# Compressed keys and values: the first layer's product in split fp32r, its weights through the shared stream

## The chip, the core and the metric

The program runs on one core of a Trainium2 chip. Its time is the device time of one execution in microseconds (us); several executions are timed and their median is given. Three runs of the kernel before gave a median of 3503.91 us (3499.05 to 3507.26).

A core has a matrix engine (TensorE; PE in the rows, with its weight loads as PEld), three engines for element-wise work (VectorE = DVE, ScalarE = ACT, GpSimd = POOL) and a queue engine (SyncE = SP) that here only issues DMAs. Each engine works through its own list of instructions in order, and an instruction that waits holds up all that stand behind it on that engine.

## The reference, cut to what matters

The program computes three layers in a row: two of a recurrent block with four kinds of mixing, and one attention layer. The change lies in the attention layer, at the place where keys and values are compressed into 15 blocks of 32 tokens:

```python
def compress(t, pe, w1, w2):
    blk = t[:, cidx] + pe[None, None, :, None, :]            # 15 blocks x 32 tokens, 4 groups
    blk = blk.transpose(0, 1, 3, 2, 4).reshape(B, n_c, G, CMP_BLOCK * dh)   # 32 x 64 = 2048 wide
    return jax.nn.gelu(blk @ w1) @ w2                        # w1: 2048 x 256, w2: 256 x 64
kc = partial_rope(compress(k_cmp, pe_ck, w_ck1, w_ck2), pos[:, cmp_end])
vc = compress(v_cmp, pe_cv, w_cv1, w_cv2)
```

`k_cmp` and `v_cmp` are two of fifteen slices of the projection `h @ w_in`. `kc` is used as extra key columns of a later attention, and `vc` as its values. The first product, `blk @ w1`, is 60 rows (4 groups x 15 blocks) by 2048 by 256, once for the keys and once for the values.

## The kernel before

**Weights.** Nearly all the products run in fp32r, a format with fewer bits than fp32. To keep the precision each operand is split into a rounded part hi and a remainder lo, and the products hi\*hi, hi\*lo and lo\*hi are summed. Activations are split once. Weights are split as they stream in, by `Core.prep` (line 82): SP loads half a megabyte into one of 3 buffers `raw` (line 102), ACT rounds it into one of 4 buffers `hi` (line 108), and DVE subtracts into one of 4 buffers `lo` (line 112). The buffers are handed out in the order in which the program calls `prep`, so the stream of weights has one order, and whoever uses a set of weights holds its buffers until then.

**Who uses the stream around the change.** Lines 174 to 176 (`stream_a`, weights as the stationary operand, 48 matmuls of 256 or 258 columns for one set of 128 outputs) and lines 225 to 227 (`stream_b`, activations stationary, 192 matmuls of 512 columns for 512 outputs over all 2048 inputs). In `block2` eight `stream_a` jobs come first and leave eight tiles `early0` to `early7`, the first four of which are `k_cmp` and `v_cmp`. Then the normalised input is split into `uq` (lines 1869 to 1871; POOL and DVE multiply into `tmp`, ACT rounds, DVE subtracts). Then come, in the order of the program: the tables for the rotary embedding (`tables`: `pos` is loaded into `pi`, DVE works out the angles at lines 1674 to 1706, ACT takes the sines at line 1705), the compression, two `stream_b` jobs for the values `vb` of the dilated attention, and the `stream_a` jobs for its queries and keys.

**Compression.** For keys and for values: ACT copies the four groups into a tile `cst` (lines 1787 and 1788, eight copies), the position term `pe` is loaded from ACT's queue (line 1790), and DVE adds it into the blocks `cbl` (line 1797, eight additions), a tile of 128 x 64 x 16, in which the 64 columns of one step j stand 16 elements apart. The weights `w1` come by ACT's queue as fp32 into buffers of their own, `cwk` and `cwv` (two each), 16 loads of 256 KB at line 1803. Line 1806 multiplies in plain fp32: for each of 16 steps j, 64 stationary columns of keys into the upper half of one PSUM bank and 64 of values into the lower half. The rest, lines 1809 to 1824, is gelu, a transposition and the second layer.

**The order of instructions.** The order on each engine isn't the order of the text. A scheduler inside the framework simulates the program and puts instructions of the engines in the order in which they become ready there, within what the data and the buffers allow. So in the program before line 1806 is spread over PE's list: 8 matmuls behind the two `vb` jobs, and 24 in small pieces between the matmuls of the next three `stream_a` jobs.

Of the kernel before, what the change touches and what calls it, by code (L numbers as in the profile page):

```python
# [9 lines left out]
F32 = mybir.dt.float32  # L10
F32R = mybir.dt.float32r
I32 = mybir.dt.int32
AF = mybir.ActivationFunctionType
OP = mybir.AluOpType
# [1696 lines left out]
class Attn:  # L1711
# [66 lines left out]
    def compress(self, xs):  # L1778

        nc, K = self.nc, self.K  # L1780
        bls = []
        for n, x in zip("kv", xs):
            st = self.t([128, 4, 256], "cst", 1)
            for g in range(4):
                src = x[g // 2]
                r = slice(64 * (g % 2), 64 * (g % 2) + 64)
                nc.scalar.copy(st[0:64, g], src[r, 0:256])
                nc.scalar.copy(st[64:128, g, 0:255], src[r, 1:256])
            pe = self.t([128, 16], "pe", 2)
            nc.scalar.dma_start(pe, self.A[f"pec{n}"])  # L1790
            bl = self.t([128, 64, 16], "cbl", 2)
            nc.gpsimd.memset(bl[:, 60:64], 0.0)
            for g in range(4):
                a = st[:, g, 0:240].rearrange("p (c j) -> p c j", j=16)[:, :, 0:16:2]
                b = st[:, g, 16:256].rearrange("p (c j) -> p c j", j=16)[:, :, 0:16:2]
                for h, v in enumerate((a, b)):
                    nc.vector.tensor_tensor(bl[:, 15 * g:15 * g + 15, 8 * h:8 * h + 8], v, pe[:, 8 * h:8 * h + 8].unsqueeze(1).to_broadcast([128, 15, 8]), op=OP.add)
            bls.append(bl)
        bank = K.g()
        for j0 in range(0, 16, 2):  # L1800
            w1 = [self.t([128, 2, 256], f"cw{n}", 2) for n in "kv"]
            for n, w in zip("kv", w1):
                nc.scalar.dma_start(w, self.A[f"wc{n}1"][:, j0:j0 + 2])
            for j in range(j0, j0 + 2):
                for i in range(2):
                    nc.tensor.matmul(bank[64 * i:64 * i + 64, 0:256], bls[i][:, :, j], w1[i][:, j - j0], start=(j == 0), stop=(j == 15))
        both = self.t([128, 4, 256], "cst", 1)
        x, u = both[:, 0], both[:, 1]
        nc.vector.tensor_copy(x, bank[:, 0:256])
        nc.vector.tensor_tensor(u, x, x, op=OP.mult)  # L1810
        nc.vector.tensor_tensor(u, u, x, op=OP.mult)
        nc.vector.scalar_tensor_tensor(u, u, 0.044715, x, op0=OP.mult, op1=OP.add)
        nc.scalar.activation(u, u, AF.Tanh, scale=math.sqrt(2.0 / math.pi))
        nc.vector.tensor_scalar(u, u, 0.5, 0.5, op0=OP.mult, op1=OP.add)
        nc.vector.tensor_tensor(x, x, u, op=OP.mult)
        for m in range(2):
            nc.tensor.transpose(bank[:, 256 + m * 128:384 + m * 128], x[:, m * 128:(m + 1) * 128], K.ident)
        hid = self.t([128, 2, 2, 64], "chid")
        nc.scalar.copy(hid, bank[:, 256:512].rearrange("p (m i c) -> p m i c", m=2, i=2))
        w2 = []  # L1820
        for n in "kv":
            w2.append(self.t([128, 2, 64], f"cw2{n}"))
            nc.scalar.dma_start(w2[-1], self.A[f"wc{n}2"])
        return hid, w2
# [330 lines left out]
```

## Time and profile before

| | before |
|---|---|
| time, median of 3 runs | 3503.91 us (3499.05 to 3507.26) |
| time of the profiled execution | 3503.24 us |
| its span, first to last instruction | 3501.4 us |
| PE busy | 3460.7 us (99%) |
| DVE busy | 2381.8 us (68%) |
| ACT busy | 1749.0 us (50%) |
| POOL busy | 492.8 us (14%) |
| DMA | 657.48 MB, mean 188 GB/s |
| granted clock of TensorE, mean | 0.994 |

Matmuls are pipelined: a row of the timeline gives a matmul's start and its own length, and the next one starts before it is over. What a matmul costs in a dense stretch is therefore the distance between two starts, not the length. The granted clock is given as a share of 2.4 GHz, so that 0.50 is 1.2 GHz. "Idle before" of a row is the time its engine did nothing ahead of it, and the arrow names what ended it. A line of the kernel before and the same line of the changed kernel differ by up to 7 in number, since the change adds 7 lines.

### The profile page before, as it was taken

The numbers are of one execution on the slowest core, as the hardware profiler recorded it, in microseconds if no ns is written. First come the engines' busy times: TensorE is split into PE (matmuls) and PEld (weight loads), VectorE is DVE, ScalarE is ACT, GpSimd is POOL, SyncE is SP. The second block draws the span as 40 slices with busy tenths as digits, with TensorE's granted clock in tenths as the row PEclk, the third lists the DMA queues.
The fourth block names the chain that finished last, engine by engine and source line by source line (L and its number), as shares of the span: only waits on it lengthen the run. The fifth ranks groups of instructions, "written<-read, shape, count | busy, mean of one in ns | idle before, by whom it ended". The sixth has DMA issues, their size and how long they took to land.

```text
span 3501.4 us, 58741 instructions
## 1 busy us (share of the span) xinstructions
PE 3460.7 (99%) x22403; PEld 2978.7 (85%) x22403; DVE 2381.8 (68%) x4330; ACT 1749.0 (50%) x2890; POOL 492.8 (14%) x686
## 2 busy tenths in 40 slices
PE   9999999999999999999999999999999999999998
PEld 8878888888888888888897888888888899988887
DVE  7776875777776546887785777776545766765554
ACT  5654544544444445655454544444345544554443
POOL 2122310211110001121320111111000112100000
PEclk9999999999999999999999999999999999999999
DMA  6334555666766665424456666666665545445555
GB/s 217 116 115 148 172 181 171 232 235 235 240 235 227 213 194 178 156 80 156 163 173 192 198 235 235 238 236 233 219 195 172 191 156 169 139 130 188 186 187 177
DMA packets 208554, 657.48 MB, mean 188 GB/s; under 512 B 24256, under 2 KB 27632, under 8 KB 208272
## 3 DMA queue, kind: packets, MB, share of 16 engines
q1 hardware_dynamic: 165952, 577.84, 50.6%
q10 hardware_dynamic: 42320, 75.89, 6.5%
q8 instruction: 176, 2.88, 0.3%
q14 instruction: 106, 0.87, 0.1%
HBM read 650.99 MB, written 2.65 MB: 187 GB/s over the span
## 4 chain that ended last, share of the span: by engine, by line
PE 95%; DVE 3%; ACT 1%; DMA 1%; issue 1%; POOL 0%; ACTq 0%; DVEq 0%; SPq 0%; POOLq 0%
PE s L178 23%; PE s L179 11%; PE s L225 8%; PE s L226 8%; PE s L227 8%; PE s L174 5%; PE s L175 5%; PE s L176 5%; PE g L225 4%; PE g L227 4%; PE g L226 4%; PE g L178 1%; PE g L175 1%; PE g L174 1%; PE g L176 1%
## 5 line engine op out<-in xcount | busy, mean ns | idle before, releaser
L112 DVE TENSOR_TENSOR lo<-raw,hi 128x1024 fp32r<-128x1024 f32 (+1 forms) x1089 | 1384.8, 1273 | 882.4 <-ACT hi L108 878.0
L108 ACT CAST hi<-raw 128x1024 fp32r<-128x1024 f32 (+1 forms) x1089 | 1139.5, 1049 | 1298.7 <-PE s L178 352.5
L178 PE MATMUL s<-uq,hi 128*128 128x512 f32 x3168 | 1111.4, 393 | 3.2 <-DVE e L276 3.2
L179 PE MATMUL s<-uq,lo 128*128 128x256 f32 x3168 | 884.2, 279 | 0.0
L178 PEld LDWEIGHTS s<-uq,hi 128*128 128x128 f32 x3168 | 593.6, 187 | 145.5 <-ACT hi L108 3.6
L179 PEld LDWEIGHTS s<-uq,lo 128*128 128x128 f32 x3168 | 593.7, 187 | 0.2
L174 PE MATMUL s<-uq,hi 128*128 128x256 f32 x1440 | 416.9, 290 | 5.2 <-ACT v L1512 2.5
L176 PE MATMUL s<-uq,lo 128*128 128x256 f32 x1440 | 416.0, 289 | 0.0
L175 PE MATMUL s<-uq,hi 128*128 128x256 f32 x1440 | 415.4, 288 | 0.0
L174 PEld LDWEIGHTS s<-uq,hi 128*128 128x128 f32 x1440 | 275.3, 191 | 14.3 <-issue 5.7
L175 PEld LDWEIGHTS s<-uq,hi 128*128 128x128 f32 x1440 | 275.1, 191 | 6.9 <-issue 6.1
L176 PEld LDWEIGHTS s<-uq,lo 128*128 128x128 f32 x1440 | 275.0, 191 | 6.8 <-issue 6.0
L226 PE MATMUL s<-lo,uq 128*128 128x512 f32 x672 | 269.4, 401 | 1.5 <-DVE lo L112 1.5
L227 PE MATMUL s<-hi,uq 128*128 128x512 f32 x672 | 267.8, 400 | 0.0
L225 PE MATMUL s<-hi,uq 128*128 128x512 f32 x672 | 266.5, 402 | 0.6 <-DVE k L1342 0.4
L444 POOL TENSOR_TENSOR gs<-e,R 128x256 f32<-128x256 f32 x88 | 77.8, 884 | 750.8 <-DVE e L276 412.9
L226 PEld LDWEIGHTS s<-lo,uq 128*128 128x128 f32 x672 | 127.4, 190 | 32.6 <-DVE lo L112 3.3
L225 PEld LDWEIGHTS s<-hi,uq 128*128 128x128 f32 x672 | 127.2, 189 | 32.0 <-issue 1.7
L227 PEld LDWEIGHTS s<-hi,uq 128*128 128x128 f32 x672 | 127.1, 189 | 30.0 <-issue 1.2
L225 PE MATMUL g<-hi,hid 128*128 128x512 f32 x352 | 139.2, 396 | 0.0
L226 PE MATMUL g<-lo,hid 128*128 128x512 f32 x352 | 139.2, 396 | 0.0
L227 PE MATMUL g<-hi,hid 128*128 128x512 f32 x352 | 139.2, 396 | 0.0
(639 smaller groups left out, 5311.2 us busy)
## 6 DMA issues: line engine op xcount, KB each, us to landing
raw<-in_wd_dram SPq DMA_DIRECT2D x176, 512.0 KB, 3.9
raw<-in_wg_dram SPq DMA_DIRECT2D x168, 512.0 KB, 4.1
raw<-in_wu_dram SPq DMA_DIRECT2D x168, 512.0 KB, 4.5
raw<-in_wina_dram SPq DMA_DIRECT2D x154, 512.0 KB, 3.8
raw<-in_win2a_dram SPq DMA_DIRECT2D x130, 512.0 KB, 3.6
raw<-in_winb_dram SPq DMA_DIRECT2D x96, 512.0 KB, 3.6
raw<-in_wout_dram SPq DMA_DIRECT2D x96, 512.0 KB, 3.9
aw<-in_wada_dram ACTq DMA_DIRECT2D x192, 256.0 KB, 4.4
```

The costliest lines, as they stand in the source:

```text
L108: self.last_hi = nc.scalar.copy(hi[:, :n], raw[:, :n])
L112: self.last = nc.vector.tensor_tensor(lo[:, :n], raw[:, :n], hi[:, :n].bitcast(F32), op=OP.subtract)
L174: nc.tensor.matmul(banks[i][:, 0:n], wh, x[:, 0:n], start=first, stop=False)
L175: nc.tensor.matmul(banks[i][:, 0:n], wh, x[:, n:2 * n], start=False, stop=False)
L176: nc.tensor.matmul(banks[i][:, 0:n], wl, x[:, 0:n], start=False, stop=last)
L178: nc.tensor.matmul(banks[i], wh, x, start=first, stop=False)
L179: nc.tensor.matmul(banks[i][:, 0:256], wl, x[:, 0:256], start=False, stop=last)
L225: nc.tensor.matmul(banks[tt], xh, wh, start=(i + j == 0), stop=False)
L226: nc.tensor.matmul(banks[tt], xh, wl, start=False, stop=False)
L227: self.last_mm = nc.tensor.matmul(banks[tt], xl, wh, start=False, stop=(end and j == 1))
L444: nc.gpsimd.tensor_tensor(g, e, rget(), op=OP.mult)
```

## The change

Four things change, all in `compress`:

- The weights `w1` no longer have buffers of their own. `K.prep` takes them, four steps j at a time: 4 sets for the keys and 4 for the values, of 512 KB each, through SP's queue and the buffers `raw`, `hi` and `lo`.
- The blocks are split as well: ACT copies `cbl`, rounded, into one half of a new tile `cb` (its name in the code is `hl`) and DVE subtracts into the other half. Both read `cbl` through the view `p c j -> p j c`, so with elements 16 apart, and write runs of 64. hi and lo of a step stand side by side as 128 stationary columns.
- For each step j there are two matmuls in fp32r, one with the hi of the weights and one with their lo, into a bank each for keys and for values: 2 x 32 in all. The upper half of the bank then holds what the blocks' hi gives and the lower half what their lo gives, and ACT and DVE add the halves together afterwards.
- Keys and values are done one after the other, where before all blocks were made first. `cbl` now has one buffer where it had two, and so has `cb`.

```diff
--- before.py
+++ after.py
@@ -1778,8 +1778,9 @@
     def compress(self, xs):
 
         nc, K = self.nc, self.K
-        bls = []
-        for n, x in zip("kv", xs):
+        banks = [K.g(), K.g()]
+        for i, n in enumerate("kv"):
+            x = xs[i]
             st = self.t([128, 4, 256], "cst", 1)
             for g in range(4):
                 src = x[g // 2]
@@ -1788,25 +1789,31 @@
                 nc.scalar.copy(st[64:128, g, 0:255], src[r, 1:256])
             pe = self.t([128, 16], "pe", 2)
             nc.scalar.dma_start(pe, self.A[f"pec{n}"])
-            bl = self.t([128, 64, 16], "cbl", 2)
+            bl = self.t([128, 64, 16], "cbl", 1)
             nc.gpsimd.memset(bl[:, 60:64], 0.0)
             for g in range(4):
                 a = st[:, g, 0:240].rearrange("p (c j) -> p c j", j=16)[:, :, 0:16:2]
                 b = st[:, g, 16:256].rearrange("p (c j) -> p c j", j=16)[:, :, 0:16:2]
                 for h, v in enumerate((a, b)):
                     nc.vector.tensor_tensor(bl[:, 15 * g:15 * g + 15, 8 * h:8 * h + 8], v, pe[:, 8 * h:8 * h + 8].unsqueeze(1).to_broadcast([128, 15, 8]), op=OP.add)
-            bls.append(bl)
-        bank = K.g()
-        for j0 in range(0, 16, 2):
-            w1 = [self.t([128, 2, 256], f"cw{n}", 2) for n in "kv"]
-            for n, w in zip("kv", w1):
-                nc.scalar.dma_start(w, self.A[f"wc{n}1"][:, j0:j0 + 2])
-            for j in range(j0, j0 + 2):
-                for i in range(2):
-                    nc.tensor.matmul(bank[64 * i:64 * i + 64, 0:256], bls[i][:, :, j], w1[i][:, j - j0], start=(j == 0), stop=(j == 15))
+
+            hl = self.t([128, 16, 2, 64], "cb", 1, F32R)
+            y = bl.rearrange("p c j -> p j c")
+            nc.scalar.copy(hl[:, :, 0], y)
+            nc.vector.tensor_tensor(hl[:, :, 1], y, hl[:, :, 0].bitcast(F32), op=OP.subtract)
+            for j0 in range(0, 16, 4):
+                hi, lo = K.prep([self.A[f"wc{n}1"][:, j0:j0 + 4].rearrange("p j c -> p (j c)")], 1024)
+                for j in range(4):
+                    for w in (hi, lo):
+                        nc.tensor.matmul(banks[i][:, 0:256], hl[:, j0 + j].rearrange("p a c -> p (a c)"), w[:, j * 256:(j + 1) * 256],
+                                         start=(j0 + j == 0 and w is hi), stop=(j0 + j == 15 and w is lo))
         both = self.t([128, 4, 256], "cst", 1)
         x, u = both[:, 0], both[:, 1]
-        nc.vector.tensor_copy(x, bank[:, 0:256])
+        for i in range(2):
+            R, Q = slice(64 * i, 64 * i + 64), slice(64 - 64 * i, 128 - 64 * i)
+            nc.scalar.copy(x[R], banks[i][Q, 0:256])
+            nc.vector.tensor_tensor(x[R], x[R], banks[i][R, 0:256], op=OP.add)
+        bank = banks[0]
         nc.vector.tensor_tensor(u, x, x, op=OP.mult)
         nc.vector.tensor_tensor(u, u, x, op=OP.mult)
         nc.vector.scalar_tensor_tensor(u, u, 0.044715, x, op0=OP.mult, op1=OP.add)
```

The scheduler then orders the instructions anew. On PE the list behind the last of the eight early `stream_a` jobs (lines 174 to 176 with 258 columns) went on with the first `vb` job (lines 225 to 227):

```order
L174 MATMUL s_27992<-u1_27386,hi_28024 128x258
L175 MATMUL s_27992<-u1_27386,hi_28024 128x258
L176 MATMUL s_27992<-u1_27386,lo_28025 128x258
L225 MATMUL s_28404<-hi_28407,uq_28057 128x512
L226 MATMUL s_28404<-lo_28408,uq_28057 128x512
L227 MATMUL s_28404<-hi_28407,uq_28057 128x512
```

At the same place all 64 new matmuls now stand (line 1808), first the 32 of the keys into bank `g_28211`, then the 32 of the values into `g_28212`, and the first `vb` job behind them; of each run of 32 the first two are shown:

```order
L176 MATMUL s_27992<-u1_27386,lo_28025 128x258
L1808 MATMUL g_28211<-hi_28238,cb_28234 128x256
L1808 MATMUL g_28211<-lo_28239,cb_28234 128x256
...
L1808 MATMUL g_28212<-hi_28318,cb_28314 128x256
L1808 MATMUL g_28212<-lo_28319,cb_28314 128x256
...
L225 MATMUL s_28462<-hi_28465,uq_28057 128x512
```

The compression's matmuls moved ahead of the 192 matmuls of `vb` (two banks of 96) that they stood behind, and no longer come in pieces. SP's list agrees: the eight loads of `w1` stand directly behind those of the early jobs and ahead of the 16 loads of `win2b`, which are the weights of `vb`.

On ACT, the stretch from the last instruction of the split of `uq` (line 1870) to the first copy of the blocks (line 1787) read as follows before; `hi<-raw` are the weights of `vb`, `vo` its result:

```order
L1870 ACTIVATE uq<-tmp,ada_94 128x256
L1670 DMA pi<-in_pos_dram 128x256
L1672 DMA ri<-in_c_rope_dram 128x4
L108 CAST hi<-raw 128x1024 x4
L1931 COPY vo<-s 128x512 x2
L108 CAST hi<-raw 128x1024 x3
L1705 ACT_TABLE_LOAD
L1705 ACTIVATE rope_28141<-tot 128x256
...
L1705 ACTIVATE rope_28173<-tx 128x256
L1787 COPY cst<-early_27371 64x256
```

Now it reads, with lines that are 1 or 7 higher, up to the rounded copy of the keys' blocks into `cb`:

```order
L1877 ACTIVATE uq<-tmp,ada_94 128x256 x7
L1670 DMA pi<-in_pos_dram 128x256
L1672 DMA ri<-in_c_rope_dram 128x4
L1705 ACT_TABLE_LOAD
L1705 ACTIVATE rope_28141<-tot 128x256
...
L1705 ACTIVATE rope_28173<-tx 128x256
L1788 COPY cst<-early_27371 64x256
...
L1791 DMA pe<-in_peck_dram 128x16
...
L1802 CAST cb<-cbl 128x16x64
```

The order of the tables, the copies and `pe` is kept. What moved is the work for `vb` (lines 108 and 1931), which has left this stretch. On DVE the eight instructions of line 112 for `vb` have left the middle of the tables' chain (lines 1674 to 1706) in the same way.

## Rows read from the trace of the kernel before

**Rows 1.** The page: busy time by engine; the chain that ended last.

```profile
PE 3460.7 (99%) x22403; PEld 2978.7 (85%) x22403; DVE 2381.8 (68%) x4330; ACT 1749.0 (50%) x2890; POOL 492.8 (14%) x686
PE 95%; DVE 3%; ACT 1%; DMA 1%; issue 1%; POOL 0%; ACTq 0%; DVEq 0%; SPq 0%; POOLq 0%
```

**Rows 2.** Timeline of PE: start us, length us, instruction, idle before and its releaser.

```profile
2738.39 0.28 PE L176 MATMUL s<-u,lo 128*128 128x258 f32 x1
2738.51 0.40 PE L225 MATMUL s<-hi,uq 128*128 128x512 f32 x1
...
2783.81 0.70 PE L1806 MATMUL g<-cwk,cbl 128*64 128x256 f32 x2
2786.93 0.45 PE L1806 MATMUL g<-cwv,cbl 128*64 128x256 f32 x1 [2.42 <-issue]
...
2790.02 0.58 PE L174 MATMUL s<-uq,hi 128*128 128x256 f32 x1 [0.62 <-ACT vo L1931]
...
2795.33 0.28 PE L175 MATMUL s<-uq,hi 128*128 128x256 f32 x1
2795.45 0.28 PE L176 MATMUL s<-uq,lo 128*128 128x256 f32 x1
```

**Rows 3.** The chain of waits around the last matmul of line 1806: start us, us.

```profile
2822.87 1.08 PE g L1806 x6
2823.94 0.31 PE s L175
```

**Rows 4.** Windows: us, busy us by engine (instructions), granted clock, DMA share, GB/s.

```profile
2790.00:2791.00 1.00, 0.98 (x4) 0.98 (x5) 1.00 (x1) 0.45 (x1) 0.00 (x0) 0.50 1.00 336
2794.00:2796.00 2.00, 2.00 (x15) 2.00 (x14) 0.00 (x0) 0.48 (x1) 0.00 (x0) 0.73 1.00 369
398.90:402.20 3.30, 3.27 (x15) 3.27 (x16) 3.30 (x6) 3.30 (x6) 0.00 (x0) 0.50 0.08 29
```

**Rows 5.** Timeline of ACT and its queue, tables and copies of the blocks.

```profile
2748.71 0.33 ACTq L1670 DMA_DIRECT2D pi<-in_pos_dram  x1
2749.61 0.50 ACT L1870 ACTIVATE uq<-tmp,ada 128x256 fp32r<-128x256 f32 x1
2774.81 0.72 ACT L1705 ACTIVATE rope<-tx 128x256 f32<-128x256 f32 x2
2775.43 0.39 ACT L1787 COPY cst<-early 64x256 f32<-64x256 f32 x1
2776.70 0.33 ACTq L1790 DMA_DIRECT2D pe<-in_peck_dram  x1
2778.39 0.40 ACT L1788 COPY cst<-early 64x255 f32<-64x255 f32 x1
```

**Rows 6.** Timeline of DVE, from the split of uq to the blocks.

```profile
2745.45 1.23 DVE L112 TENSOR_TENSOR lo<-raw,hi 128x1024 fp32r<-128x1024 f32 x1 [0.48 <-ACT hi L108]
2748.25 0.42 DVE L1869 TENSOR_TENSOR tmp<-hs,R 128x256 f32<-128x256 f32 x1
2752.56 0.29 DVE L1674 CAST pf<-pi 128x256 f32<-128x256 int32 x1 [1.02 <-DMA pi<-in_pos_dram]
2752.77 1.22 DVE L112 TENSOR_TENSOR lo<-raw,hi 128x1024 fp32r<-128x1024 f32 x1
2753.91 0.61 DVE L1686 TENSOR_SCALAR ang<-pf,ri 128x256 f32<-128x256 f32 x2
...
2772.87 1.21 DVE L112 TENSOR_TENSOR lo<-raw,hi 128x1024 fp32r<-128x1024 f32 x1
2781.45 1.64 DVE L1797 TENSOR_TENSOR cbl<-cst,pe 128x120 f32<-128x120 f32 x8 [5.28 <-DMA pe<-in_peck_dram]
```

**Rows 7.** Groups of the whole program by shape: busy us, mean ns of one.

```profile
L108 ACT CAST hi<-raw 128x1024 fp32r<-128x1024 f32 x1086 | 1137.2, 1049 | 1294.0 <-PE s L178 352.5 <-PE s L227 263.7 <-PE g L227 200.7
L112 DVE TENSOR_TENSOR lo<-raw,hi 128x1024 fp32r<-128x1024 f32 x1086 | 1382.2, 1275 | 875.9 <-ACT hi L108 871.5 <-PE g L227 0.5 <-PE g L480 0.2
```

**Rows 8.** DMA issues, 2720 to 2830 us: KB each, median us to landing.

```profile
raw<-in_win2b_dram SPq DMA_DIRECT2D x16, 512.0 KB, 3.6
cw2k<-in_wck_dram ACTq DMA_DIRECT2D x1, 64.0 KB, 1.8
```

**Rows 9.** Weight loads of line 1806 (ns min/median/max), and those of line 178.

```profile
L1806 PEld LDWEIGHTS g<-cwk,cbl x32: 184/201/227, 2783.8 to 2822.9; 128*64 128x64 f32 x32
L178 PEld LDWEIGHTS s<-uq,hi 128*128 128x128 f32 x3168 | 593.6, 187 | 145.5 <-ACT hi L108 3.6
```

**Rows 10.** Waits of PE, whole program: us in total, times, longest.

```profile
PE s L174 <- ACT q L1888: 2.1, 1, 2.1
```

## The prediction

> **What bounds the kernel now.** I read the page first. PE is busy for 99% of the span, and the chain that ended last runs on PE for 95% of it [rows 1]. So time is won only where PE does less, and whatever makes PE wait is paid in full unless another wait goes for it. The next question is what the compression costs on PE today. I take it from PE's timeline as a balance over one stretch, since busy times of pipelined matmuls overlap.
>
> The stretch begins at 2738.51 us, when the eight early jobs are over and the first `vb` matmul starts, and ends at 2823.94 us, when the last matmul of line 1806 is over [rows 2, 3]: 85.43 us. By the order of the instructions it holds 192 matmuls of `vb`, 160 of the next `stream_a` jobs and all of line 1806. The 192 took 2783.81 - 2738.51 = 45.30 us [rows 2]. The 160, had they run as the dense ones do, 0.12 us from start to start (2795.33 to 2795.45, [rows 2]), would take 19.2 us. The rest, 85.43 - 45.30 - 19.2 = **20.9 us**, is what the compression costs on PE now: its matmuls, 2.42 us of waiting for the values' blocks, 0.62 us for a bank [rows 2], the changes between the two kinds of matmul, and a slow clock after the wait: the granted clock is 0.50, the lower level of 1.2 GHz, at 2790 to 2791 us and comes back between 2794 and 2796 us [rows 4].
>
> **What goes.** The 20.9 us go. With them go 16 DMA issues from ACT's queue (line 1803); ACT is busy half the time [rows 1] and the issues lie beside PE's work, so I count nothing.
>
> **What is added on PE.** 64 matmuls of 256 columns in fp32r. The nearest rows are those of lines 175 and 176 with the same 256 columns and 128 stationary ones, 0.12 us apart [rows 2]: 3.85 us for the keys, 3.85 us for the values. On ACT and DVE come two roundings, two subtractions and small additions, priced below where they stand in PE's way.
>
> **What is moved, and here the sum is decided.** Before, line 1806 stood behind `vb`. Its operands came late, but PE had 45 us of `vb` to do until then. Now the weights of the compression are ahead of those of `vb` in the stream, the 64 matmuls stand ahead of `vb` on PE, and PE works in order. Behind them wait not only `vb` but all that follows. So the cover is gone, and I have to work out when the keys' split blocks are there. PE is free at 2738.51 us; nothing says that the blocks will be.
>
> The chain to them is the one of before, with less in between. (1) The tables begin when `pi` has landed. Its load is issued behind the last step of the split of `uq`: the last `tmp` at 2748.25 us, the load at 2748.71, the first use at 2752.56, for which DVE had waited [rows 5, 6]. One instruction of line 112 that stood ahead of that `tmp` on DVE (2745.45, 1.23 us, [rows 6]) is gone, so I take 1.2 us off. (2) The tables' chain on DVE had eight instructions of line 112 inside it, the first at 2752.77 and the last at 2772.87 us [rows 6]; each held the next one up for 1.14 us (2752.77 to 2753.91, [rows 6]). They leave: 9.1 us off. (3) The sines, then the eight copies follow as before: the last two sines at 2774.81, first copy at 2775.43, last copy done at 2778.79, the position term issued at 2776.70 us [rows 5]. All this moves 10.3 us ahead: copies done at 2768.5, `pe` issued at 2766.4. (4) The additions for the keys took 1.64 us and began at 2781.45, when `pe` had landed 4.75 us after its issue [rows 5, 6]. Before, four loads of 256 KB followed it on the queue. Now only small ones do, and of those the load of `cw2k` landed in 1.8 us [rows 8]. Between 1.8 and 4.75 I take 3.3 us, so the additions begin at 2769.7 us (bounds 2768.5, when the copies are done, and 2771.15) and end at 2771.3. (5) The rounding on ACT and the subtraction on DVE, both of 128x1024: 1.05 and 1.27 us by lines 108 and 112 [rows 7]. The first matmul can start at about 2773.7 us, bounds 2772.5 and 2775.1.
>
> So PE waits 2773.7 - 2738.5 = **35.2 us** ahead of the keys.
>
> A second wait stands between keys and values. `cb` has one buffer, so the values' rounding can't begin until the last of the keys' matmuls, and on ACT it also stands behind three roundings of the values' weights, the third of which needs a `hi` buffer that the keys' 24th matmul frees. From that matmul: 1.05 + 1.05 + 1.27 = 3.4 us, less the eight matmuls that PE still has (1.0 to 1.7 us, dense or at the lower clock): about **2.0 us**.
>
> After each wait the clock is low. After 2.54 us of idle time at 398.9 us the granted clock was 0.50 until 402.2 [rows 4], and 15 matmuls of 256 columns took these 3.3 us, 0.22 apart where 0.12 is dense: 1.5 us lost. After the 2.42 us wait it was low from 2790.0 at the latest to about 2795.1 us (a mean of 0.73 over the last window, [rows 4]): 5.1 us, some 23 matmuls, 2.3 us lost. The keys' 32 matmuls, all of them slow, would lose 3.0 us. For the two waits together I take 4.0 us, bounds 1.5 and 6.
>
> Sum on PE after: 35.2 + 3.85 + 2.0 + 3.85 + 4.0 = 48.9 us, against 20.9 us before: **28.0 us more**. The profiled execution took 3503.24 us, its span 3501.4; the 1.8 us around it stay. 3503.24 + 28.0 = 3531.2, so **3531 us**. The profiled execution is within 0.7 us of the median of the runs, so this stands for the median too.
>
> **A rule that speaks against the split itself.** Rounding and subtraction read `cbl` with elements 64 bytes apart. No row of ACT or DVE reads that way. The nearest is PE's weight load from that same tile, 64 columns in 201 ns where 128 columns that lie together take 187 [rows 9]: per column twice as long at most, a part of it being fixed. So the two of each of keys and values cost between nothing and 2 x (1.05 + 1.27) = 4.6 us more, all of it in PE's two waits. I take nothing: line 1797 reads 8 bytes apart and takes 1.64 us / 8 / 120 = 1.7 ns an element, and line 1869, whose elements lie together, 0.42 us / 256 = 1.6 ns [rows 6]. I keep 4.6 for the range. The Trainium skill, "SBUF — State Buffer", Specifications (TRN2), says that SBUF is read in lines of 16 bytes, that at least two accesses must fall in one line for full bandwidth, and that each crossing costs something; it gives no price. By that rule the 4.6 us end would be the nearer one, and the sum 3536 us.
>
> **The rivals.**
>
> *Not slower, the operands are early.* The place is ACT's list ahead of the first copy (line 1787). The copies need only `early0` and `early1`, not the tables, and if they were done while the early jobs still ran, PE would hardly wait: 3.85 + 2.0 + 3.85 = 9.7 us against 20.9, so 3503.24 - 11.2 = **3492 us**. It decides at the wait ahead of the keys: below 35.2 - 28.0 = 7.2 us, with the first new matmul before 2745.7 us, the change is not slower. For it speaks that the copies' own inputs are ready before 2738 us. Against it, that ACT is in order and the copies stand behind the sines in its list, the sines behind DVE's angles, and these behind `pi`, which was issued at 2748.71 us [rows 5]. That alone is past the point. 3 in 100.
>
> *The split reads slowly* (the rule above): 28.0 + 4.6, **3536 us**. 15 in 100. It would show in the two instructions' own lengths.
>
> *The stream starts again slowly.* While PE waits, three `raw` buffers are full and no load can be issued until a subtraction frees one; a load takes 3.6 us to land [rows 8], then 1.05 and 1.27 us [rows 7]: 5.9 us for three buffers is 2.0 us a set, faster than the 2.8 us of `vb` per set (45.30 / 16). But the first sets come one after the other and PE may wait 1 to 3 us more, 2 by the middle: **3533 us**. 12 in 100.
>
> *The loss comes back later*, since ACT and DVE get ahead while PE waits. What could come back is PE's idle time, and the largest single wait behind this stretch is 2.1 us [rows 10]: **3529 us** at the best. 10 in 100. Both cases lie in my range.
>
> *The change doesn't do what it says*: the instructions are all there in the new order, in the number worked out above; nothing for it.
>
> **How the numbers follow.** My forecast, 3531 us, has 60 in 100, and the four cases above 40. Low end: 28.0 - 1.2 (blocks early) - 2.5 (clock) - 2.1 (a wait gone) = 22.2, and 4 us for the spread of the runs shown (3499.05 to 3507.26): 3521. High end: 28.0 + 1.4 (blocks late) + 2 (clock) + 4.6 (slow reads) + 2 (slow start) = 38.0 and 4: 3545. About 8 in 10 lie between; the rest is the early case and an error in the chain of more than these bounds. A measurement of this kernel can tell about 0.2%, 7 us, from no change. Every case but the first is beyond that on the slow side: slower 95 in 100, the same 2, faster 3.
>
> **What would show it.** PE idle for about 35 us ahead of the first row of line 1808, released by DVE's subtraction into `cb`; line 1808's first row at about 2774 us, `vb`'s first behind it at some 2787; a second idle of 2 to 3 us in the middle of the 64; a granted clock of 0.50 in the keys' matmuls. The tables without line 112 among them, some 10 us sooner than now. Wrong is the prediction if the idle ahead of the keys is under 7.2 us, if PE has `vb` ahead of the 64, or if the stretch from 2738.5 us to the first `vb` matmul is far from 49 us.

## The result, and the profile after

| | before | after |
|---|---|---|
| time, median of 4 runs each on the same chip | 3504.57 us (3499.05 to 3507.26) | 3530.09 us (3529.22 to 3534.26) |
| ratio after / before, with 95% interval | | 1.008 (1.0069 to 1.0092) |
| profiled execution, its span | 3503.24, 3501.4 us | 3530.69, 3528.9 us |
| PE busy | 3460.7 us (99%) | 3454.0 us (98%) |
| granted clock, mean | 0.994 | 0.990 |

The kernel became 25.5 us slower. Two lines of the page after answer to [rows 1]: busy time by engine, and the chain that ended last.

```profile
PE 3454.0 (98%) x22403; PEld 2978.5 (84%) x22403; DVE 2391.7 (68%) x4341; ACT 1761.2 (50%) x2902; POOL 508.2 (14%) x686
PE 94%; DVE 4%; ACT 1%; DMA 1%; issue 1%; POOL 0%; DVEq 0%; ACTq 0%; SPq 0%; POOLq 0%
```

PE has 6.7 us less work and the time is longer all the same: it waits. The page's second part, the span in 40 slices, shows where (PE, and its granted clock):

```profile
PE   9999999999999999999999999999999599999998
PEclk9999999999999999999999999999999799999999
```

One slice of 88 us has a 5, and a 7 for the clock. The list of PE's waits (us in total, times, longest) is headed by it. The 2.1 us of [rows 10] no longer stand in it.

```profile
PE g L1808 <- DVE cb L1803: 37.8, 2, 33.7
PE g L369 <- DMA h<-in_x_dram: 4.1, 2, 3.4
PE s L174 <- ACT v L1512: 3.1, 1, 3.1
```

PE's timeline, which answers to [rows 2] and [rows 3], has the two waits and the pace of the products:

```profile
2740.07 0.28 PE L176 MATMUL s<-u,lo 128*128 128x258 f32 x1
2774.08 0.58 PE L1808 MATMUL g<-hi,cb 128*128 128x256 f32 x1 [33.74 <-DVE cb L1803]
2774.46 0.41 PE L1808 MATMUL g<-lo,cb 128*128 128x256 f32 x1
2774.68 0.41 PE L1808 MATMUL g<-hi,cb 128*128 128x256 f32 x1
...
2778.44 0.28 PE L1808 MATMUL g<-hi,cb 128*128 128x256 f32 x1
2778.56 0.28 PE L1808 MATMUL g<-lo,cb 128*128 128x256 f32 x1
...
2784.07 0.38 PE L1808 MATMUL g<-hi,cb 128*128 128x256 f32 x1 [4.03 <-DVE cb L1803]
...
2789.48 0.62 PE L225 MATMUL s<-hi,uq 128*128 128x512 f32 x2
```

Four windows cut the stretch at these points (us, busy us by engine with instructions, granted clock, DMA share, GB/s), to be read beside [rows 4]:

```profile
2740.19:2774.08 33.89, 0.15 (x2) 0.00 (x1) 24.11 (x73) 15.04 (x29) 8.14 (x14) 0.56 0.18 52
2774.08:2780.04 5.96, 5.96 (x32) 5.75 (x32) 4.18 (x10) 4.35 (x7) 0.15 (x1) 0.64 0.10 30
2780.04:2784.07 4.03, 0.00 (x1) 0.00 (x1) 3.18 (x3) 3.29 (x4) 0.00 (x0) 1.00 0.86 281
2784.07:2789.48 5.41, 5.41 (x32) 5.41 (x33) 3.85 (x4) 2.50 (x3) 0.00 (x0) 0.68 0.57 176
```

33.89 us of waiting, 5.96 us for the keys' products, 4.03 us of waiting, 5.41 us for the values': 49.3 us, where the kernel before spent 20.9. That is 28.4 more. The span grew by 27.5: this execution came to the stretch 1.7 us later than the one of before, and some 2.6 us were made up behind it, most of it the 2.1 us wait. The medians differ by 25.5, 2.0 less than the spans, since the profiled execution of before lies 1.3 us below its median and the one of after 0.6 above.

The chain to the keys' blocks, on ACT and its queue and on DVE, answers to [rows 5] and [rows 6]. DVE's part of the tables ran in one piece, with no row of line 112 among it.

```profile
2748.75 0.33 ACTq L1670 DMA_DIRECT2D pi<-in_pos_dram  x1
2764.80 0.72 ACT L1705 ACTIVATE rope<-tx 128x256 f32<-128x256 f32 x2 [1.18 <-DVE tx L1704]
2765.43 0.39 ACT L1788 COPY cst<-early 64x256 f32<-64x256 f32 x1
2766.68 0.34 ACTq L1791 DMA_DIRECT2D pe<-in_peck_dram  x1
2770.19 1.91 ACT L1802 CAST cb<-cbl 128x1024 fp32r<-128x1024 f32 x1 [1.44 <-DVE cbl L1798]
2780.12 1.97 ACT L1802 CAST cb<-cbl 128x1024 fp32r<-128x1024 f32 x1
```

```profile
2751.95 0.29 DVE L1674 CAST pf<-pi 128x256 f32<-128x256 int32 x1 [2.18 <-DMA pi<-in_pos_dram]
2768.44 1.64 DVE L1798 TENSOR_TENSOR cbl<-cst,pe 128x120 f32<-128x120 f32 x8 [3.47 <-DMA pe<-in_peck_dram]
2772.13 1.90 DVE L1803 TENSOR_TENSOR cb<-cbl,cb 128x1024 fp32r<-128x1024 f32 x1 [2.05 <-ACT cb L1802]
```

### The profile page after: what moved, and what is told of

It reads as the page before. It is cut to its first block, busy times and chain, and to the rows that moved or that the text cites. A ratio compares the mean times of both kernels' runs of the same rounds, so it can differ in the third digit from the quotient of the medians.

```text
span 3528.9 us, 58763 instructions
## 1 busy us (share of the span) xinstructions
PE 3454.0 (98%) x22403; PEld 2978.5 (84%) x22403; DVE 2391.7 (68%) x4341; ACT 1761.2 (50%) x2902; POOL 508.2 (14%) x686
## 4 chain that ended last, share of the span: by engine, by line
PE 94%; DVE 4%; ACT 1%; DMA 1%; issue 1%; POOL 0%; DVEq 0%; ACTq 0%; SPq 0%; POOLq 0%
PE s L178 23%; PE s L179 11%; PE s L225 8%; PE s L226 8%; PE s L227 7%; PE s L174 5%; PE s L176 5%; PE s L175 5%; PE g L225 4%; PE g L227 4%; PE g L226 4%; PE g L178 1%; DVE lo L112 1%; PE g L175 1%; PE g L174 1%
## 5 line engine op out<-in xcount | busy, mean ns | idle before, releaser
L444 POOL TENSOR_TENSOR gs<-e,R 128x256 f32<-128x256 f32 x88 | 85.4, 971 | 743.1 <-DVE e L276 405.9
L227 PE MATMUL g<-hi,hid 128*128 128x512 f32 x352 | 139.2, 396 | 0.0
L225 PE MATMUL s<-hi,hid 128*128 128x512 f32 x352 | 139.2, 396 | 0.0
L226 PE MATMUL s<-lo,hid 128*128 128x512 f32 x352 | 139.2, 396 | 0.0
```

What stands on the lines that cost most here:

```text
L225: nc.tensor.matmul(banks[tt], xh, wh, start=(i + j == 0), stop=False)
L226: nc.tensor.matmul(banks[tt], xh, wl, start=False, stop=False)
L227: self.last_mm = nc.tensor.matmul(banks[tt], xl, wh, start=False, stop=(end and j == 1))
L444: nc.gpsimd.tensor_tensor(g, e, rget(), op=OP.mult)
```

## The experiments

The theory: the loss comes from the place of the products, which stand ahead of all that could cover the chain to the blocks. The first rival: the split itself is dear (64 products with 128 columns, roundings and subtractions of blocks and weights), wherever it stands. A second question was whether the split's reads, 64 bytes apart, cost what the trace suggests. Differences below are between medians, each beside the kernel before on the same chip.

**One and two jobs of `vb` ahead of the compression.** In the first run the call stands behind both jobs, in the second between them.

```diff
+    vb = K.t(oo, [128, 2, 1024], "vo", 1)
+    ob = K.t(oo, [128, 2, 1024], "ob")
+    for h in range(2):
+        run_b(lambda tt, bank, h=h: nc.scalar.copy(vb[:, tt, h * 512:(h + 1) * 512], bank))
     cc = ExitStack()
     ...
-    vb = K.t(oo, [128, 2, 1024], "vo", 1)
-    ob = K.t(oo, [128, 2, 1024], "ob")
-    for h in range(2):
-        run_b(lambda tt, bank, h=h: nc.scalar.copy(vb[:, tt, h * 512:(h + 1) * 512], bank))
```

> The changed kernel with one move: the call of the compression stands behind both vb jobs in the text, so its weights come behind those of vb in the stream, as its matmuls stood in the kernel before. Arithmetic, buffers and the second wait are kept. Theory (the place in the stream exposes a wait of 34 us that vb's 45 us had covered): the wait ahead of the keys falls from 33.7 us to 0 to 2 us, since eight subtractions for vb come back into the tables' chain (9 us) and PE comes by 45 us later; left are 7.7 us of matmuls, the second wait of about 4 us and some 3.5 us of slow clock, 15 to 17 us against 20.9 in the kernel before: 3498 to 3502 us. Rival (the split itself is dear: 64 matmuls, roundings at 1.9 us, a slow clock): place does not matter much, 3520 us or more.

> The changed kernel with the call of the compression between the two vb jobs: half of the cover. Theory: PE comes to the first new matmul 22.6 us later, and four subtractions for vb (4.6 us) come back into the chain, so the wait ahead of the keys falls by 18 us to about 16 us: 3512 us, between the changed kernel and the one with both jobs ahead. Rival (the split is dear wherever it stands): 3520 us or more, and no difference of 10 us or more between this and the run with both jobs ahead.

Behind both: 3503.82 us against 3503.13, ratio 0.9998 (0.9989 to 1.0008). Behind one: 3515.53 us, ratio 1.0035 (1.0022 to 1.0048). PE's waits for the blocks in the two, first behind both, then behind one:

```profile
PE g L1808 <- DVE cb L1803: 8.6, 2, 5.5
```

```profile
PE g L1808 <- DVE cb L1803: 22.6, 2, 18.6
```

The keys' wait is 33.7 us with no job of `vb` ahead, 18.6 with one and 3.1 with two (8.6 less 5.5). With the same split the loss is gone when the cover is back, so the place decides and the first rival falls. Both times lie above what was expected, 1.8 us above 3502 and 3.5 above 3512, since the keys' wait came out some 1 to 3 us longer. And nothing was gained: behind both jobs the stretch of the compression still takes 21.6 us, about what the kernel before spends, since three waits (3.1, 0.7 and 5.5 us) and a granted clock of 0.76 have come to 7.7 us of products:

```profile
2785.08:2806.66 21.58, 12.29 (x66) 11.77 (x67) 15.27 (x20) 15.50 (x21) 0.15 (x1) 0.76 0.61 204
```

**The order alone.** The arithmetic of the kernel before, in fp32 with 64 stationary columns and no split; only its weights come through the stream's `raw` buffers.

```diff
-            w1 = [self.t([128, 2, 256], f"cw{n}", 2) for n in "kv"]
+            w2 = K.t(K.wp, [128, 1024], "raw", 3).rearrange("p (i j c) -> p i j c", i=2, j=2)
+            w1 = [w2[:, 0], w2[:, 1]]
             for n, w in zip("kv", w1):
-                nc.scalar.dma_start(w, self.A[f"wc{n}1"][:, j0:j0 + 2])
+                nc.sync.dma_start(w, self.A[f"wc{n}1"][:, j0:j0 + 2])
```

> The kernel before with its plain fp32 matmuls, and only the buffers of its weights changed: w1 is loaded unsplit into the three buffers raw of the stream, from the sync engine's queue, so that the 32 fp32 products come ahead of vb. No rounding, no subtraction, no fp32r, and both cbl buffers kept. Theory: PE waits some 34 us for the values' blocks as in the changed kernel, then 11 to 17 us of products (partly at the lower clock): 3526 to 3538 us. Rival (the split is what costs): 3502 to 3506 us, as before.

3528.62 us, ratio 1.0074 (1.0057 to 1.009). PE's timeline (start, length, idle before and what ended it):

```profile
2762.48 1.09 PE L1807 MATMUL g<-raw,cbl 128*64 128x256 f32 x2 [25.58 <-issue]
2766.41 6.62 PE L1807 MATMUL g<-raw,cbl 128*64 128x256 f32 x30 [2.85 <-issue]
...
2783.07 0.73 PE L225 MATMUL s<-hi,uq 128*128 128x512 f32 x2 [2.27 <-ACT hi L108]
```

The profile names nothing that ended the 25.58 us, but DVE's row does: the eight additions for the keys run until then.

```profile
2760.93 1.64 DVE L1797 TENSOR_TENSOR cbl<-cst,pe 128x120 f32<-128x120 f32 x8 [3.52 <-DMA pe<-in_peck_dram]
```

The keys' wait is 8.2 us shorter than the changed kernel's, where the same 34 us were expected: no split follows the additions, and they begin 4 us earlier, as `pi` is issued 4.6 us after PE is free (8.6 in the changed kernel). The fp32 products and the smaller waits among them make up for it.

So the loss comes without any split at all. It is the stream's buffers that carry the products ahead of `vb`: whoever takes a buffer of the stream takes a place in its order, and PE has to use it before what is queued behind it. (The loads also go to SP's queue in place of ACT's; no run parts the two.)

**The call ahead of the tables.** Here the chain to the blocks is shortened instead. The compression's memory lies where the tables' working tiles lie, so those, and `pe`, had to give up their second buffers too.

```diff
+    cp = pool("cmp", "right", cc)
+    T.pool = cp
+    hid, w2 = T.compress((tiles[0:2], tiles[2:4]))
     T.pool = ap
...
     tabA, tabB = tables(K, ap, A)
...
-            a = K.t(tp, [128, 256], "ang", 2)
+            a = K.t(tp, [128, 256], "ang", 1)
```

> The changed kernel with the compression called ahead of the rotary tables in the text, so that its tiles lie elsewhere and ACT makes the copies of the blocks directly behind the split of uq, not behind the sines (to fit, the tables' work tiles and the position term have one buffer each). Place in the stream, arithmetic and the second wait are kept. Theory: the wait is the chain to the blocks and shrinks with it; copies from about 2750 us, first new matmul at about 2759 us where the changed kernel has 2774, wait 19 us in place of 33.7: 3515 us. Rival (the split is dear, the chain does not matter): 3527 to 3533 us. Second rival (another input, the weights, is late as well): wait over 25 us, 3521 us or more.

3517.93 us, ratio 1.0042 (1.0027 to 1.0057), and the keys' wait is 19.4 us, as expected; the time is 2.9 us above the 3515 expected. The 14 us less are what `pi`, the tables' arithmetic and the sines put into the chain. My prediction said that the copies need the early tiles and not the tables. By the kernel's text they also need memory that the tables' working tiles held, which I didn't see. The run moves the memory and ACT's list together, so which of the two held the copies isn't shown.

**The block tile laid out position first**, so that the split reads values that lie together.

```diff
-            bl = self.t([128, 64, 16], "cbl", 1)
+            bl = self.t([128, 16, 64], "cbl", 1)
...
-            y = bl.rearrange("p c j -> p j c")
+            y = bl
```

> The changed kernel with the block tile laid out position first (16 x 64 instead of 64 x 16), so that the cast and the subtraction of the split read consecutive values instead of every sixteenth; place and order stay. If the strided reads are what makes the split dearer than the nearest rows (1.91 and 1.90 us against 1.05 and 1.27 of the same size in the stream), the two fall to about 1.05 and 1.27, each of the two waits shrinks by 1.5 us (33.7 to 32.2, 4.0 to 2.5) and the time falls by 3.0 to about 3527. If the cost lies in the interleaved writing or the fp32r output (which stay), nothing changes: 3530. The adds that fill the tile then write at a stride of 64 elements and read at one of 16; if that is dear, their 8 x 205 ns grow and eat the gain.

3526.55 us against 3502.55, ratio 1.0067 (1.0054 to 1.0079): a loss of 24.0 us where the changed kernel's is 25.5. That is 1.5 us of gain where 3.0 were expected, which the times can't tell from 3.0 or from nothing; the rows tell more. ACT's and DVE's rows, with the additions of the keys:

```profile
2767.54 1.04 ACT L1802 CAST cb<-cbl 128x1024 fp32r<-128x1024 f32 x1 [2.10 <-DVE cbl L1798]
```

```profile
2765.24 2.18 DVE L1798 TENSOR_TENSOR cbl<-cst,pe 128x120 f32<-128x120 f32 x8 [3.59 <-DMA pe<-in_peck_dram]
2768.61 1.23 DVE L1803 TENSOR_TENSOR cb<-cbl,cb 128x1024 fp32r<-128x1024 f32 x1 [1.19 <-ACT cb L1802]
```

Cast and subtraction fall from 1.91 and 1.90 to 1.04 and 1.23 us, so the stride was the cause, and the interleaved writing costs nothing. The additions now read 64 bytes apart in turn, and grow from 1.64 to 2.18 us for eight. Their own lengths (ns, shortest, median and longest), first in the kernel before, then here:

```profile
L1797 DVE TENSOR_TENSOR cbl<-cst,pe x16: 275/279/284, 2781.4 to 2786.7; 128x120 f32<-128x120 f32 x16
L1798 DVE TENSOR_TENSOR cbl<-cst,pe x16: 343/350/364, 2765.2 to 2772.1; 128x120 f32<-128x120 f32 x16
```

The keys' wait falls by 1.0 us to 32.7 (1.54 less, 0.54 more), the values' by 1.6 to 2.4, where the additions are off the path. Of these 2.6 us the keys' products took 0.9 back: 6.82 us at a granted clock of 0.54, against 5.96 at 0.64.

**Both edits**, the place behind `vb` and the new layout (the two edits above together).

> The compression behind both jobs of vb and the position-first block tile. Of the run with the place alone (3503.8: waits of 3.1, 0.7 and 5.5, and a stretch of 21.6 us for 7.7 us of products at the full clock, 0.76 granted), the strided reads should take 1.5 off the first and 1.5 off the third wait: about 3500.5 if the slow clock stays, some 4 us less (3496) if waits this short no longer bring it. If the place alone decides and the split's reads lie beside other work: 3503.5 as there.

3501.45 us against 3502.55, ratio 0.9995 (0.9985 to 1.0004): 1 us above the 3500.5 expected with a slow clock, and within what can't be told from no change. The keys' wait is 2.75 us, 0.3 less where 1.5 were expected; the values' is 3.97, 1.5 less as expected; the granted clock is 0.66 in the compression's 20 us.

**Weights in buffers of the compression's own**, at the changed kernel's place.

```diff
-            for j0 in range(0, 16, 4):
-                hi, lo = K.prep([self.A[f"wc{n}1"][:, j0:j0 + 4].rearrange("p j c -> p (j c)")], 1024)
-                for j in range(4):
+            for j0 in range(0, 16, 2):
+                raw, hi, lo = self.t([128, 512], "cw", 1), self.t([128, 512], "cwh", 1, F32R), self.t([128, 512], "cwl", 1, F32R)
+                nc.scalar.dma_start(raw, self.A[f"wc{n}1"][:, j0:j0 + 2].rearrange("p j c -> p (j c)"))
+                nc.scalar.copy(hi, raw)
+                nc.vector.tensor_tensor(lo, raw, hi.bitcast(F32), op=OP.subtract)
+                for j in range(2):
```

> The changed kernel with the weights loaded and split in buffers of the compression's own instead of the stream's, at the same place in the text; eight sets of two positions for each of keys and values. The products are then bound to no place in the stream, and stand between those of the jobs that follow. If the tie to the stream's buffers causes the loss, the wait of 33.7 goes: no wait on the blocks above 3 us, 7.7 us of products against the 20.9 of the kernel before, less the waits for single sets: 3494 to 3502. If the split itself (128 columns, two passes, cast and subtraction) causes it, it stays near 3525.

3536.17 us, ratio 1.0095 (1.0082 to 1.0109): a miss, and slower than the changed kernel. The wait of 33.7 us did go, as `vb` moved ahead (the first product stands at 2787.28 us, behind it), but other waits came:

```profile
PE g L1811 <- ACT cwh L1807: 21.3, 8, 4.7
PE g L1811 <- DVE cb L1803: 4.0, 1, 4.0
PE g L1827 <- DVE cst L1825: 3.5, 1, 3.5
```

Each kind has one buffer, so every set went through load, cast and subtraction one after the other; ACT's rows of two sets in a row show the step:

```profile
2839.76 0.33 ACTq L1806 DMA_DIRECT2D cw<-in_wcv_dram  x1
2842.51 0.62 ACT L1807 CAST cwh<-cw 128x512 fp32r<-128x512 f32 x1 [3.50 <-DMA cw<-in_wcv_dram]
2843.88 0.34 ACTq L1806 DMA_DIRECT2D cw<-in_wcv_dram  x1
```

4.1 us a set, of which PE fills 1.7. The run changes several things at once: the tie to the stream, the depth of the buffers, the size of a set and the queue. That `vb` moved ahead fits the theory. That the stream's three `raw` buffers are what was missing is likely by these rows, but not shown by a run of its own.

**Blocks first.** The keys' blocks made ahead of `vb`, the products behind it, the split blocks in halves with three buffers, position first.

```diff
+    keys = T.compress_prep(tiles[0:2], "k")
... (the two jobs of vb)
+    hid, w2 = T.compress((tiles[0:2], tiles[2:4]), keys)
...
+            hl = self.t([128, 8, 2, 64], "cb", 3, F32R)
```

> As the run with both changes, but the keys' blocks are made and split ahead of the two jobs of vb (the products stay behind them), and the split blocks come in halves of eight positions in three buffers, so that the first half of the values' blocks is made while the keys' products run. If waits on the blocks, and the slow clock behind an idle TensorE, are all that the compression costs beyond its products, then 20.9 us become 7.7 plus waits of 0 to 3 us at the full clock: 3490 to 3494, faster than both kernels. If 64 products in one piece bring the slow clock by themselves, 4 us more: 3494 to 3498. If the earlier casts and adds delay the splits of vb's weights, waits appear inside vb and the gain is eaten: 3500 or above.

3501.71 us against 3502.55, ratio 0.9997 (0.9988 to 1.0006): a miss again, and not by the reason given for 3500 and above, since no wait stands inside `vb`. The wait on the blocks is down to 1.42 us, but the weights' own splits are now the limit. PE's timeline, five of the eight waits:

```profile
2788.18 0.38 PE L1812 MATMUL g<-hi,cb 128*128 128x256 f32 x1 [1.42 <-DVE cb L1798]
...
2792.10 0.38 PE L1812 MATMUL g<-lo,cb 128*128 128x256 f32 x1 [1.12 <-DVE lo L112]
...
2793.77 0.39 PE L1812 MATMUL g<-lo,cb 128*128 128x256 f32 x1 [0.46 <-DVE lo L112]
...
2795.51 0.39 PE L1812 MATMUL g<-lo,cb 128*128 128x256 f32 x1 [0.52 <-DVE lo L112]
...
2797.91 0.39 PE L1812 MATMUL g<-lo,cb 128*128 128x256 f32 x1 [0.88 <-DVE lo L112]
```

A set of four positions takes 1.23 us on DVE and gives PE 8 products of 0.12 us, 0.96. In one piece the products can't run faster than the split. The granted clock is 0.82 over the whole: 1.00 up to 2797.91 us, 0.53 behind it. Whether the waits alone lower it, or the products in one piece as well, this run doesn't part:

```profile
2786.77:2804.70 17.93, 12.36 (x65) 10.40 (x66) 14.06 (x21) 12.10 (x19) 0.25 (x2) 0.82 0.67 212
```

**Spread.** As with the blocks first, but the eight sets go to the stream one at a time, one ahead of each job of q and k of heads 2 to 5; the sums of keys and values share one bank, and the rest of the compression comes ahead of head 6. Then, once more, with ScalarE's copies for the blocks queued behind the last eviction of `vb`. In that second run the first set also comes three jobs later, at k of head 3 (its expectation says one job and q), and the rest at head 7.

```diff
+    def a_job(name):
+        T.pool = cp
+        next(steps, None)
+        T.pool = ap
+        return run_a(name, 2)
... (the second run)
+    with tc.issue_after(moved[-1].ins):
+        keys = T.compress_prep(tiles[0:2], "k")
...
+        if next(count) >= 3:
+            next(steps, None)
```

> As the run with the blocks first, but the eight sets of weights are handed to the stream one at a time, one ahead of each of the jobs of q and k of heads 2 to 5, so that 8 products of 0.12 us stand between jobs whose products cover the cast and the subtraction of the set (1.05 and 1.23 us a set, against 0.96 us of products). In that run the products in one piece met seven waits of 0.2 to 1.1 us on the splits of the weights, beside one of 1.4 on the blocks. If these waits and the slow clock are what is left of the cost, all of it goes but the 7.7 us of products: 20.9 become 8 to 10 and the time 3490 to 3493, faster than both kernels. If VectorE and ScalarE, which have the heads' softmax in the same stretch, fall behind by each set's 1.2 us, the waits come back on the splits of q and k: 3496 to 3503.

> As the run with the sets spread, but ScalarE's copies for the blocks are queued behind the eviction of vb's second half, and the first set of weights stands one job later (ahead of k of head 2 it was; now q of head 3). In the run before, one wait of 7.2 us was left: the first product of q found no free bank of sums, since the eviction of vb stood in ScalarE's queue behind the blocks' copies and casts, which waited for the 128 x 16 encodings and for the adds. If that wait is what is left to gain, it goes whole: 3496.9 less 7 is 3490. If the copies then hold up what stands behind them (the softmax of heads 0 and 1, the casts of the weights of q and k), part of it comes back as a wait of 2 to 5 us in the same place: 3492 to 3495.

The first: 3496.91 us against 3503.03, ratio 0.9985 (0.9976 to 0.9994). That is above the 3490 to 3493 expected. All waits inside the products are gone, though the first two sets still stand together on PE, and one wait stood in a new place:

```profile
PE s L174 <- ACT vo L1923: 7.2, 1, 7.2
```

The eviction of `vb` stood behind the blocks' copies on ACT, and the first job of q had no bank to write to. The second: **3491.34 us against 3503.74, ratio 0.996 (0.9947 to 0.9974)**, faster than both kernels, and between its two expectations. Its longest wait near the compression (2802.25 us), and a window from ahead of it to past the last product of line 1813 (2863.1 us), are:

```profile
PE s L174 <- ACT q L1903: 1.2, 1, 1.2
```

```profile
2800.00:2881.00 81.00, 79.79 (x664) 79.13 (x663) 62.12 (x130) 50.45 (x92) 17.17 (x12) 1.00 0.66 206
```

All runs but the one with own buffers on one scale: what the compression cost PE in the trace (its waits and the length of its products, slow clock included), less the 20.9 us of before, and the measured difference of the medians. In the two spread runs the cost is 7.7 us of products and the wait for a bank; in the first of them a granted clock of 0.98 over the next 87.8 us adds 1.8.

| run | waits for blocks and weights | cost on PE | less 20.9 | measured |
|---|---|---|---|---|
| changed kernel | 33.9 + 4.0 | 49.3 | +28.4 | +25.5 |
| order alone | 25.6 + 2.9 + 1.4 + 2.8 | 46.9 | +26.0 | +25.5 |
| position first | 32.7 + 2.4 | 47.6 | +26.7 | +24.0 |
| ahead of the tables | 19.4 + 4.3 | 36.5 | +15.6 | +14.8 |
| behind one job | 18.6 + 4.0 | 35.1 | +14.2 | +12.4 |
| behind both | 3.1 + 0.7 + 5.5 | 21.6 | +0.7 | +0.7 |
| both edits | 2.8 + 4.0 | 20.0 | -0.9 | -1.1 |
| blocks first | 5.6 | 17.9 | -3.0 | -0.8 |
| spread | 7.2 (a bank) | 16.7 | -4.2 | -6.1 |
| spread, behind the eviction | 1.2 (a bank) | 8.9 | -12.0 | -12.4 |

The two columns agree to 2.9 us; where a wait of 18 us or more stands, the measured loss is 0.5 to 2.9 us smaller. The 2.1 us wait of [rows 10] is gone from its place in all these runs, so it doesn't tell them apart, and the costs come from one execution each, which lies up to 3.4 us from its median (both edits: 3498.09 against 3501.45). What makes up the rest stays open.

## Why the prediction held, and which terms were off

The mechanism was the one forecast: PE idle ahead of the first row of line 1808 until DVE's subtraction into `cb`, with `vb` queued behind. The time, 3530.09, is 0.9 us from the 3531 forecast, and that near partly by luck: the first wait came out 1.3 us shorter, the second 2.0 longer, the clock 0.3 cheaper, and the 1.7 us by which this execution came late and the 2.6 made up behind the stretch went against each other. The terms, counted from when PE is free (2738.51 before, 2740.19 in this execution), were less exact than their sum:

| term | forecast | measured |
|---|---|---|
| `pi` issued | 9.0 | 8.6 |
| first use of `pi` on DVE | 12.9 | 11.8 |
| last sines | 26.0 | 24.6 |
| additions for the keys begin | 31.2 | 28.3 |
| first product of the keys (the wait) | 35.2 | 33.9 |
| second wait | 2.0 | 4.0 |
| slow clock, both blocks of products | 4.0 | 3.7 |
| products at full clock | 7.7 | 7.7 |
| sum | 48.9 | 49.3 |

*The landing of `pe`* was over-sized: 3.3 us, taken between 1.8 and 4.75; it was in use 1.76 us after its issue (2766.68 to 2768.44). My reason for a shorter landing, that only small loads follow it on its queue, was wrong too: in the runs with the compression behind `vb` the queue is the same, and it was in use 3.8 to 4.9 us after its issue there. What goes with the short landing in each run is a stream that stands still. Windows from the issue to the first use, in the changed kernel, in the one ahead of the tables, in the one with both edits and in the kernel with the blocks first (the last columns are the clock, the DMA share and GB/s):

```profile
2766.68:2768.44 1.76, 0.00 (x0) 0.00 (x0) 0.00 (x1) 1.69 (x5) 1.69 (x3) 0.50 0.10 9
```

```profile
2752.82:2754.59 1.77, 0.00 (x0) 0.00 (x0) 0.29 (x2) 1.70 (x5) 0.00 (x0) 0.50 0.16 36
```

```profile
2773.96:2778.88 4.92, 4.92 (x23) 3.95 (x22) 0.00 (x0) 4.01 (x7) 2.15 (x4) 1.00 0.62 197
```

```profile
2779.07:2782.99 3.92, 3.92 (x18) 3.15 (x17) 0.00 (x0) 3.82 (x7) 2.15 (x4) 1.00 0.72 227
```

While PE waits, the stream's buffers are full, few loads run, and the small load is fast. So the wait I computed seems to shorten its own chain, which I hadn't seen; no run varies the traffic alone. With `pi` 0.7 us faster as well (3.2 us from issue to use, against 3.85 by [rows 5, 6]) and issued 0.4 earlier, the additions began 2.9 us earlier than forecast, and 1.7 earlier than the lower of my bounds (30.0): they didn't wait for the last copy, which ended 0.3 us after they began.

*The split* was under-sized: 1.05 and 1.27 us by [rows 7], measured 1.91 and 1.90, so 1.5 us more ahead of each block of products. This was the rival "the split reads slowly", priced at no more than 4.6 us for all four; it came to 3.0. I had taken the rows of 8-byte steps as the nearest, and they weren't: 64 bytes was the size that mattered, and the layout run shows it. I had also set a distance between starts (1.64 us / 8) beside line 1869's own length. By lengths, 1.23 us for 1024 elements that lie together and 0.42 us for 256 give 0.28 us for 120, an estimate from [rows 6], and an addition at 8-byte steps takes 0.279: that conclusion stands. The rule of the Trainium skill, "SBUF — State Buffer", Specifications (TRN2), that two accesses should fall in one line of 16 bytes, agrees with this trace: steps of 8 bytes cost nothing [rows 6], steps of 64 bytes some 0.7 to 0.9 us in 1024 elements. So its warning was right and my choice of row wrong, but the error was hidden by that on `pe`.

*The second wait* was 4.0 us: the 2.0 forecast, 1.5 for the slow split, and 0.5 that my sum had lost. ACT's third rounding of the values' weights ended at 2780.05 and the keys' products at 2780.04, so the rounding into `cb` could begin only there (2780.12). Rounding and subtraction behind that point are 2.3 us by [rows 7], more than the 2.0 taken, though I had said that the rounding waits for the last product; 0.2 us of steps between the instructions are the rest.

*The clock*: nineteen of the keys' products start 0.21 us apart where 0.12 is dense (granted 0.64 over that window), the values' block slows only after its first eight products. 5.96 and 5.41 us for 3.85 each: 2.1 + 1.6 = 3.7 us lost, near the 4.0 taken.

*The loss comes back later* was a rival of 10 in 100. The 2.1 us of [rows 10] are gone, in the size given, but they are gone from their place in every run, also where no wait was longer than 5.5 us (behind both jobs), so the reason I gave, PE's long wait, isn't shown. *The stream starts again slowly* didn't come true: `vb` runs dense from its first row on, since the stream had refilled during the values' products. *The operands are early* fell with the wait of 33.9 us, but its place could be tried: even ahead of the tables the keys' wait is 19.4 us, far past the 7.2 us from which that rival decides.

## What to carry to other kernels

A load that moves into a shared, ordered stream of buffers takes its consumer along in the order; before such a move, work out when the *other* operand of that consumer will be there, and what the engine has to do until then. Cheaper products gain nothing in a lump: here 64 products that take 7.7 us cost 18 to 22 us in one piece, by waits on blocks, waits on the splits of weights and a slow clock, and 9 when spread, most of them in eights or less and the first 16 together, between jobs that cover their splits. A term that is hard to price should be bounded by a row that shares its stride, not only its size.

## What the runs showed of the hardware

- Reads 64 bytes apart: 1.91 to 1.97 us on ACT and 1.90 on DVE for 128x1024 in fp32, against 1.04 and 1.23 for the same work on elements that lie together; DVE's additions of 128x120 went from 279 to 350 ns (medians) when they read 64 instead of 8 bytes apart.
- The granted clock falls to the lower level (0.50, 1.2 GHz) for part of the time behind short waits too. Means: 0.64 over the keys' products behind 33.7 us, 0.68 over the values' behind 4.0 us (the first eight still at full pace), 0.76 over 21.6 us with waits of 3.1, 0.7 and 5.5 us; behind the single wait of 1.2 us in the last run a mean of 1.00 was granted.
- The same load of 8 KB was in use 1.7 to 1.9 us after its issue where the DMA share was 0.16 or less (five runs), and 3.8 to 4.9 us after it where the share was 0.54 to 0.92 (0.92 in the kernel before), whatever followed on its own queue.
